# A two-layer decoder trunk: the entries of its feed-forward layers reordered (squares added on VectorE, two raw pairs in layer 1, the first scaled pair's weights of layer 0 held in token tiles)

## The chip, the cores and the metric

One Trainium2 chip, one core of it. The metric is the device time in microseconds (us) of one execution, the median of three runs. Engines: TensorE (PE, with its weight loads PEld), VectorE (DVE), ScalarE (ACT), GpSimd (POOL), SyncE (SP). Each engine works through a queue of its own, in order, and waits on semaphores for the others; most DMAs are issued from SP's queue, some from POOL's.

## The reference, cut to what matters

A residual stream h of 512 tokens by 1024 features goes through two layers. In layer 0 the mixer is a retention and an mLSTM head group (`ab_mixer`), in layer 1 a sparse attention with compressed, selected and window branches (`nsa_mixer`). Each layer then has the same two steps:

```python
for i in range(DEPTH):
    h = h + mixer_i(rms_norm(h, ...), ...)
    h = h + conv_ffn(rms_norm(h, ffn_norm_g[i]), ffn_w_up[i], ffn_conv_w[i], ffn_conv_b[i], ffn_w_down[i])
    e = rms_norm(p[i] @ ple_w[i], ple_norm_g[i])
    gate = sigmoid(rms_norm(h, ple_gate_norm_g[i]) @ ple_w_gate[i])
    h = h + gate * e

def conv_ffn(h, w_up, conv_w, conv_b, w_down):
    a, b = split(h @ w_up, 2)              # 1024 -> 2 x 2816
    a = causal_dwconv(a, conv_w, conv_b)   # width 3 over tokens
    return (gelu(a) * b) @ w_down
```

`rms_norm` divides each token by the root of the mean of its squares, so a product of *unnormalised* (raw) tokens with a weight can be multiplied by the token's factor afterwards.

## The kernel before, in words

Features lie on the partitions, tokens along the free axis: h is eight tiles `self.h[k]` of 128 x 512 (in the trace `hp`, or `h`). Every float32 product is made of three matmuls, `mm3` (L176 to L178): operands are split into a high and a low part, high by a copy on ACT (L136, `split`), low by a subtraction on DVE (L137); then high x high, low x high, high x low go into the same PSUM tile. So each weight tile passes through a raw tile `wr` (four buffers; the load waits until the buffer is free), then `wh` (ACT) and `wl` (DVE). `load` (L159) issues the load under a high priority, and where its caller stands in the code decides together with that priority where it comes in the queues: the order of each engine's queue is worked out ahead of time, by a scheduler that simulates a timeline. `self.behind(engine)` pins an instruction behind the last one traced on that engine. `y` tiles are 28 token tiles of 128 x 512, `sc` tiles six of scratch, `g` tiles twenty in the feed-forward layer.

A norm has these steps: `acc_square` squares each h tile on ACT (L232) and adds it into `acc`, seven adds, six on POOL and the last on DVE (L234); `norm_sum` transposes acc on PE (L310), sums on DVE (L311) and takes an inverse root by small operations (L215 to L221); `norm_cast` spreads it over the partitions by PE (L324) into `n.b` (in the trace `rb`). The raw tokens' parts `norm_parts` are a copy on ACT (L244) and a subtraction on DVE (L245); the normalised tokens are made by `scaled_tokens` (L262 to L275: `fh`, `fl`, `gh`, `gl`, `y`).

**Layer 0, from the mixer into the feed-forward layer.** The mixer's output goes through w_abo in two halves; the second half is eight pieces m of 12 matmuls (`out_piece`, with `out_products`, L370 ff.), and each adds into h[m] on DVE (L373). Ahead of it stand the last head group's products, finished on DVE (L545) after a spread on PE (L324). Behind it `begin` squares and adds h, and fills PE with products of the embedding: p (`pT`, loaded and split in `Embed.fill`) by w_ple, eight pieces of six matmuls, with `norm_sum` after the third and `norm_cast` after the sixth. Then the first pair of up-products (f=0) begins, its two products interleaved with an offset of 2.5 steps.

**Feed-forward layers.** There are 22 blocks f, each a pair of up-products. Blocks below `PLAINS[i]` are plain: 2 x 24 matmuls of 512 columns (`mm_up`). The others (`up`) use a product scheme of seven instead of eight: 84 matmuls of 256 columns, whose operand forms DVE prepares (`forms`) and whose weight sums come by accumulating DMAs from POOL's queue (L1489, L1496: `ep`, `es`; ACT and DVE split the sums into `eh`, `el`). Each block is convolved and gated (`conv`, L1452 to L1455, `act_up`), and groups of blocks (`PARTS`) are multiplied down into h (`down`, L1562).

**Layer 1.** All eight embedding products are done within the attention's steps (750 to 920 us), so at the entry there is nothing to fill with. Instead the first pair (f=0) is multiplied with raw tokens: six of the eight steps of a, `norm_sum`, the others, four steps of b, `norm_cast`, the rest; a is multiplied by `n.b` on DVE (L1466), the gated result once more on POOL (L1469).

**The attention's entry** (633 to 720 us) starts with a norm (`norm_in`), the products of keys, values and gate columns (L803 transposes the gates after L797 on ACT), and the hidden steps of the compressed blocks (L877, L878). In the steps behind it, L1070 to L1126, an order by a planner is interleaved with the output products.

Of the kernel before, what the change touches and what calls it, by code (L numbers as in the profile page):

```python
# [20 lines left out]
P = 128  # L21
# [21 lines left out]
PLAINS = (5, 6)  # L43
# [20 lines left out]
class Trunk:  # L64
# [73 lines left out]


# [96 lines left out]
    def norm_step(self, n, c0, k, place=None):  # L236
        self.norm_parts(n, c0, k, place)
        self.acc_square(n, k, self.h[k])
# [10 lines left out]
    def norm_in(self, c0, place=None):  # L249
        n = Norm()  # L250
        for k in range(KD):
            self.norm_step(n, c0, k, place)
        return n
# [120 lines left out]

    def out_proj(self, src, half, oh, ol):
        for m in range(KD):
            self.out_piece(src, half, m, oh, ol)


    def ab_mixer(self):  # L380
        nc, I, tc = self.nc, self.I, self.tc
        with ExitStack() as ctx:
# [357 lines left out]
            self.out_proj(I["w_abo"], 1, [h for h, _ in mo], [l for _, l in mo])  # L740
        return self.Embed(self, 0, None, self.dram.tile([D, T], F32, name="emb0"), 0)


    def nsa_mixer(self):
# [4 lines left out]
        with ExitStack() as ctx:  # L749
# [18 lines left out]
            n = self.norm_in(C_NSA)  # L768
# [429 lines left out]
            hidden_step(1, xv, ph, 1)  # L1198
            key_stack(1, keys[1])
            q1 = self.Tokens(self, I["w_q"][1], n)  # L1200
            q1.steps(0, 1)
            key_stack(2, keys[2])
# [24 lines left out]
            emb = self.Embed(self, 1, lambda m: self.y().bitcast(F32), self.dram.tile([D, T], F32, name="emb"), KD)  # L1227
# [100 lines left out]
            for m in range(KD):  # L1328
                embed(m, EMBED_AT[m])
                out_first(m, OUT_AT[m])  # L1330
# [32 lines left out]
            for m in range(KD):  # L1363
                if m % 2 == 0:
                    if m // 2 + 4 not in wo:
                        wo[m // 2 + 4] = self.load(I["w_nso"][1, m // 2])
                self.out_add(m, self.out_products(wo[m // 2 + 4], m, *outs[1]))
        return emb


    def ffn(self, i, e):
        nc, I, tc = self.nc, self.I, self.tc
        plain = PLAINS[i]
        with ExitStack() as ctx:
# [23 lines left out]

            def begin():
                self.cycle = ("a", "b")  # L1400
                if e.done == KD:
                    n = Norm()
                    for k in range(KD):
                        self.acc_square(n, k, self.h[k])
                        self.norm_parts(n, C_FFN + 8 * i, k, g_tile)
                    ws = [self.load(I["w_up"][i, x]) for x in (0, NF)]
                    first = [self.bank() for _ in ws]
                    for step, (x, ks) in enumerate(((0, range(6)), (0, range(6, KD)), (1, range(4)), (1, range(4, KD)))):
                        with self.behind(*[nc.tensor] * (step > 0)):
                            for k in ks:  # L1410
                                s = slice(k * P, (k + 1) * P)
                                self.mm3(first[x], ws[x][0][:, s], ws[x][1][:, s], n.h[k], n.l[k], k == 0, k == KD - 1)
                        if step in (0, 2):
                            with self.behind(nc.tensor):
                                (self.norm_sum if step == 0 else self.norm_cast)(n)
                    n.h, n.l = [], []
                    ws = [self.load(I["w_up"][i, x]) for x in (1, NF + 1)]
                    self.scaled_tokens(n, C_FFN + 8 * i, places, whole)
                    return n, ws, first
                n = Norm()  # L1420
                for k in range(KD):
                    self.acc_square(n, k, self.h[k])
                fill = e.fill(g_tile)
                jobs = fill[:3] + [lambda: self.norm_sum(n)] + fill[3:6] + [lambda: self.norm_cast(n)] + fill[6:]
# [3 lines left out]
                ws = [self.load(I["w_up"][i, x]) for x in (0, NF)]  # L1428
                self.scaled_tokens(n, C_FFN + 8 * i, places, whole)
                return n, ws, None  # L1430
# [3 lines left out]
            def mm_up(f):  # L1434
                self.cycle = ("a", "b")
                if f > (first is not None):
                    return self.ws(I["w_up"][i, f], n), self.ws(I["w_up"][i, NF + f], n)
                ps = [self.bank() for _ in ws]
                order = sorted([(k, 0, k) for k in range(KD)] + [(k + 2.5, 1, k) for k in range(KD)])
                for step, (_, x, k) in enumerate(order):  # L1440
                    s = slice(k * P, (k + 1) * P)
                    with self.behind(*[nc.tensor] * (step > 0)):
                        self.mm3(ps[x], ws[x][0][:, s], ws[x][1][:, s], n.h[k], n.l[k], k == 0, k == KD - 1)
                return ps
# [17 lines left out]
            def act_up(f, pa, pb):  # L1462
                raw = first is not None and f == 0
                if raw:
                    a, pa = pa, a_tile()
                    nc.vector.tensor_tensor(pa, a, n.b, ALU.mult)  # L1466
                c = conv(f, pa)
                if raw:
                    nc.gpsimd.tensor_tensor(c, c, n.b, ALU.mult)  # L1469
                nc.vector.scalar_tensor_tensor(c, pb, -1.0, c, ALU.mult, ALU.mult)  # L1470
                keep(f, c)
# [93 lines left out]
            act_up(0, *(first or mm_up(0)))  # L1565
            jobs = []
            for f in range(1, NF):
                if f < plain:
                    if f == plain - 1:
                        with tc.high_priority(offset=AHEAD):  # L1570
                            ahead[0].load()
                            ahead[0].open()
                    act_up(f, *mm_up(f))
                else:
                    up(f)
                if f == 1:
                    forms = self.forms(n)
                if forms:
# [13 lines left out]
    class Embed:  # L1592
        def __init__(self, trunk, i, place, away, done):
            self.k, self.i, self.place, self.away, self.done = trunk, i, place, away, done
            self.n, self.e = Norm(), []

        def fill(self, tile):
            tr = self.k
            src = tr.I["pT"][self.i]
            raw = tr.wp.tile([P, 1024], F32, name=tr.nm("wr"), tag="wr", bufs=4)  # L1600
            self.p = [[tile(), tile()], [tile(), tile()]]
            with tr.tc.high_priority(offset=AHEAD):
                tr.nc.sync.dma_start(raw, src)
                for k in range(2):
                    tr.split(self.p[0][k], self.p[1][k], raw[:, k * T : k * T + T])
            self.place = lambda m: tile().bitcast(F32)
            ws = {}
# [193 lines left out]
```

## Time and profile before

| | |
|---|---|
| median of three runs | 1347.6 us (1346.89 to 1347.86) |
| the profiled execution's own time | 1348.33 us |
| its span, first to last instruction | 1346.5 us |
| mean granted clock of PE | 0.997 |
| PE busy | 1325.0 us, 7826 matmuls |
| DVE, ACT, POOL busy | 1015.0, 739.4, 376.3 us |
| bytes moved by DMA | 171.69 MB, 128 GB/s on average |

The stages by the timeline: the first mixer to about 204 us (its last products run into the entry of the feed-forward layer, first up-product at 239.6), feed-forward layer 0 to 600, its gate to 633, attention to 925, feed-forward layer 1 to 1313, its gate to the end.

How to read it: a line of a timeline has its start, its duration, the engine, the line of the kernel, the operation, output <- inputs, and in brackets how long the engine had been idle and what ended that. "x3" are three in a row. In the list of waits "a <- b" is what waited and what it waited for. Busy times are of the profiled execution.

### The profile page before, as it was taken

The numbers are of one execution on the slowest core, as the hardware profiler recorded it, in microseconds if no ns is written. First come the engines' busy times: TensorE is split into PE (matmuls) and PEld (weight loads), VectorE is DVE, ScalarE is ACT, GpSimd is POOL, SyncE is SP. The second block draws the span as 40 slices with busy tenths as digits, with TensorE's granted clock in tenths as the row PEclk, the third lists the DMA queues.
The fourth block names the chain that finished last, engine by engine and source line by source line (L and its number), as shares of the span: only waits on it lengthen the run. The fifth ranks groups of instructions, "written<-read, shape, count | busy, mean of one in ns | idle before, by whom it ended". The sixth has DMA issues, their size and how long they took to land.

```text
span 1346.5 us, 21190 instructions
## 1 busy us (share of the span) xinstructions
PE 1325.0 (98%) x7826; PEld 1148.3 (85%) x7826; DVE 1015.0 (75%) x1658; ACT 739.4 (55%) x1310; POOL 376.3 (28%) x399
## 2 busy tenths in 40 slices
PE   9999999999999999999999999999899999999998
PEld 7888877789999999888788888887689999999887
DVE  6866866787888877678777878766897788877675
ACT  5357524555555555355466888664454555555342
POOL 3356423011111110331422887673100111110320
PEclk9999999999999999999999999999999999999999
DMA  6532344555666553333243322114255666653421
GB/s 239 159 100 94 110 127 157 176 149 160 173 175 174 145 140 91 129 114 118 85 154 113 111 65 56 28 52 109 83 172 144 169 174 172 164 135 91 133 97 63
DMA packets 72191, 171.69 MB, mean 128 GB/s; under 512 B 8468, under 2 KB 15252, under 8 KB 72088
## 3 DMA queue, kind: packets, MB, share of 16 engines
q1 hardware_dynamic: 62296, 152.91, 35.6%
q0 software_dynamic: 9504, 17.31, 7.8%
q8 instruction: 61, 1.00, 0.3%
q14 instruction: 42, 0.34, 0.1%
q10 hardware_dynamic: 288, 0.14, 0.0%
HBM read 148.29 MB, written 7.35 MB: 116 GB/s over the span
## 4 chain that ended last, share of the span: by engine, by line
PE 91%; DVE 3%; ACT 2%; DMA 1%; issue 1%; POOL 1%; ACTq 0%; POOLq 0%; DVEq 0%
PE ps L176 26%; PE ps L177 26%; PE ps L178 26%; PE ps L1126 3%; PE ps L1101 3%; PE ps L1070 2%; PE ps L1071 1%; DMA es<-in_w_up_dram 1%; ACT wh L136 1%; PE ps L459 1%; DVE wl L137 1%; PE ps L1072 1%; PE ps L310 1%; POOL acc L234 1%; PE ps L996 1%
## 5 line engine op out<-in xcount | busy, mean ns | idle before, releaser
L136 ACT ACTIVATE wh<-wr 128x1024 fp32r<-128x1024 f32 (+2 forms) x182 | 186.7, 1029 | 223.1 <-PE ps L177 169.4
L177 PE MATMUL ps<-y,wh 128*128 128x512 f32 (+1 forms) x752 | 264.2, 352 | 0.2 <-DVE y L137 0.2
L176 PE MATMUL ps<-y,wh 128*128 128x512 f32 (+1 forms) x752 | 263.1, 355 | 1.0 <-ACT y L136 0.9
L178 PE MATMUL ps<-y,wl 128*128 128x512 f32 (+1 forms) x752 | 262.5, 352 | 0.0
L137 DVE TENSOR_TENSOR wl<-wr,wh 128x1024 fp32r<-128x1024 f32 (+2 forms) x165 | 203.0, 1231 | 67.0 <-ACT wh L136 65.9
L176 PEld LDWEIGHTS ps<-y,wh 128*128 128x128 f32 x752 | 142.9, 190 | 22.7 <-ACT y L136 1.6
L177 PEld LDWEIGHTS ps<-y,wh 128*128 128x128 f32 x752 | 142.8, 190 | 19.4 <-DVE y L137 0.6
L178 PEld LDWEIGHTS ps<-y,wl 128*128 128x128 f32 x752 | 142.8, 190 | 18.4
L177 PE MATMUL ps<-g,wh 128*128 128x512 f32 x384 | 150.8, 393 | 2.6 <-DVE g L245 2.6
L176 PE MATMUL ps<-g,wh 128*128 128x512 f32 x384 | 150.9, 393 | 0.0
L178 PE MATMUL ps<-g,wl 128*128 128x512 f32 x384 | 150.0, 391 | 0.0
L1489 POOL DMA_DIRECT2D ep<-ep x33 | 28.4, 861 | 278.4 <-DMA ep<-in_w_up_dram 129.0
L1496 POOL DMA_DIRECT2D es<-in_w_up_dram x33 | 29.0, 887 | 254.6 <-DVE sc L1453 149.7
L177 PEld LDWEIGHTS ps<-g,wh 128*128 128x128 f32 x384 | 72.6, 189 | 17.5 <-DVE g L245 3.9
L234 POOL TENSOR_TENSOR acc<-acc,sc 128x512 f32<-128x512 f32 x36 | 58.1, 1614 | 104.0 <-ACT sc L232 102.9
L1562 DVE TENSOR_TENSOR hp<-hp,ps 128x512 f32<-128x512 f32 x96 | 65.6, 683 | 26.8 <-PE ps L178 26.8
L178 PEld LDWEIGHTS ps<-g,wl 128*128 128x128 f32 x384 | 72.4, 189 | 15.2
L1086 POOL TENSOR_SCALAR pr<-pr,sm,gate 128x512 f32<-128x512 f32 (+3 forms) x128 | 76.4, 614 | 29.5 <-DVE sm L1084 22.5
L176 PEld LDWEIGHTS ps<-g,wh 128*128 128x128 f32 x384 | 72.7, 189 | 14.1
L1529 ACT ACTIVATE sc<-ps 128x256 f32<-128x256 f32 x132 | 50.1, 380 | 60.7 <-PE ps L178 58.8
L176 PE MATMUL ps<-y,gh 128*128 128x256 f32 x264 | 75.0, 284 | 0.0
L178 PE MATMUL ps<-y,fl 128*128 128x256 f32 x264 | 74.8, 283 | 0.0
(366 smaller groups left out, 3388.4 us busy)
## 6 DMA issues: line engine op xcount, KB each, us to landing
wr<-in_w_up_dram SPq DMA_DIRECT2D x55, 512.0 KB, 3.7
ep<-in_w_up_dram SPq DMA_DIRECT2D x33, 512.0 KB, 5.6
wr<-in_w_down_dram SPq DMA_DIRECT2D x64, 256.0 KB, 3.0
es<-in_w_up_dram SPq DMA_DIRECT2D x33, 256.0 KB, 2.9
es<-in_w_up_dram POOLq DMA_DIRECT2D x33, 256.0 KB, 6.4
ep<-ep POOLq DMA_DIRECT2D x33, 256.0 KB, 3.8
wr<-in_w_plg_dram SPq DMA_DIRECT2D x16, 512.0 KB, 3.7
wr<-in_w_down_dram SPq DMA_DIRECT2D x32, 192.0 KB, 2.9
```

What stands on the lines that cost most here:

```text
L136: self.nc.scalar.activation(hi, src, AF.Copy)
L137: (eng or self.nc.vector).tensor_tensor(lo, src, hi.bitcast(F32), ALU.subtract)
L176: mm(out, ah, bh, start=first, stop=False, **kw)
L177: mm(out, ah, bl, start=False, stop=False, **kw)
L178: mm(out, al, bh, start=False, stop=last, **kw)
L234: eng.tensor_tensor(n.acc, n.acc, sq, ALU.add)
L1086: nc.gpsimd.tensor_scalar(prs[b], prs[b], sm[:, b : b + 1], gate[:, j, hd, 1 + b : 2 + b], ALU.mult, ALU.mult)
L1101: nc.tensor.transpose(pt[:, n * w + i * P : n * w + (i + 1) * P], pr[:, n, i * P : (i + 1) * P], self.ident)
L1126: nc.tensor.matmul(po[0:m, cols], vv[i][:, b, g, 0:m], src, start=False, stop=last and b == 1 and i == 0 and part == 0)
L1496: nc.gpsimd.dma_start(me.s3, I["w_up"][i, me.f][:, :T], accum_op=ALU.add)
L1529: copy = lambda out, ps: nc.scalar.activation(out, ps, AF.Copy)
L1562: nc.vector.tensor_tensor(self.h[m], self.h[m], ps, ALU.subtract)
```

## The change

1. **Squares.** `acc_square` gets VectorE for all its adds at the entries of both feed-forward layers and of the attention; POOL no longer adds there. The first mixer and the gates keep POOL.
2. **Layer 0.** Four steps move from the entry in between the pieces of the second half of w_abo (`ahead`): after piece 0 the load and split of pT (`Embed.parts`), after 2 the first half of w_ple (`Embed.weights`), after 4 and 6 the two weights of the first scaled pair (`whole_y`), which are now split into eight y tiles instead of `wh` and `wl`. The first pair is interleaved with an offset of half a step.
3. **Layer 1.** Two pairs (f=0 and 1, `RAW = 2`) are multiplied with raw tokens, their weights loaded by `load_now`. `norm_sum` comes after the second of the four products, `norm_cast` after the third. All four products are multiplied by n.b on DVE. `PLAINS` is (5, 7), so f=6 becomes plain. One embedding product (m=7, `LEFT = 1`) is left for the entry, with pT and w_ple loaded again between the last output products of the attention.
4. **Others.** The forms start four blocks ahead of the first seven-product block; in the attention's entry the gate columns stand behind the first step of q0, and a hidden step behind the first step of q1.

The diff, cut to its core:

```diff
-PLAINS = (5, 6)
+PLAINS = (5, 7)
+RAW = 2
+LEFT = 1
...
+    def whole_y(self, src):
+        raw = self.wp.tile([P, 1024], F32, name=self.nm("wr"), tag="wr", bufs=4)
+        with self.tc.high_priority(offset=AHEAD):
+            self.nc.sync.dma_start(raw, src)
+        halves = []
+        for x in range(2):
+            hi, lo = self.y(), self.y()
+            self.split(hi, lo, raw[:, x * T : x * T + T])
+            halves.append((hi, lo))
+        return [halves[k // 4][c][:, k % 4 * P : k % 4 * P + P] for c in range(2) for k in range(KD)]
...
-            n = self.norm_in(C_NSA)
+            n = self.norm_in(C_NSA, eng=nc.vector)
...
-            self.out_proj(I["w_abo"], 1, [h for h, _ in mo], [l for _, l in mo])
-        return self.Embed(self, 0, None, self.dram.tile([D, T], F32, name="emb0"), 0)
+            e = self.Embed(self, 0, None, self.dram.tile([D, T], F32, name="emb0"), 0)
+            ahead = {0: e.parts, 2: e.weights, 4: lambda: e.up.append(self.whole_y(I["w_up"][0, 0])), 6: lambda: e.up.append(self.whole_y(I["w_up"][0, NF]))}
+            for m in range(KD):
+                self.out_piece(I["w_abo"], 1, m, [h for h, _ in mo], [l for _, l in mo])
+                if m in ahead:
+                    ahead[m]()
+        return e
...
-            gate_columns(sg)
             xv = blocks(1, hT[1])
             q0 = self.Tokens(self, I["w_q"][0], n)
             q0.steps(0, 1)
+            gate_columns(sg)
...
-            emb = self.Embed(self, 1, lambda m: self.y().bitcast(F32), self.dram.tile([D, T], F32, name="emb"), KD)
+            emb = self.Embed(self, 1, lambda m: self.y().bitcast(F32), self.dram.tile([D, T], F32, name="emb"), KD - LEFT)
...
+                if m in (4, 6):
+                    (emb.parts if m == 4 else emb.weights)()
...
             def begin():
                 self.cycle = ("a", "b")
-                if e.done == KD:
-                    n = Norm()
+                n, raw = Norm(), Norm()
+                if e.done:
+                    ws = {}
                     for k in range(KD):
-                        self.acc_square(n, k, self.h[k])
-                        self.norm_parts(n, C_FFN + 8 * i, k, g_tile)
...
+                        self.norm_parts(raw, C_FFN + 8 * i, k, g_tile)
+                        if k == 3:
+                            ws[0, 0] = parts_of(self.load_now(I["w_up"][i, 0]))
+                    for f, x in ((0, 1), (1, 0)):
+                        with self.behind(nc.vector):
+                            ws[f, x] = parts_of(self.load_now(I["w_up"][i, x * NF + f]))
                 for k in range(KD):
-                    self.acc_square(n, k, self.h[k])
...
+                    self.acc_square(n, k, self.h[k], nc.vector)
+                if e.done:
+                    ws[1, 1] = parts_of(self.load_now(I["w_up"][i, NF + 1]))
+                    first = [[self.bank(), self.bank()] for f in range(RAW)]
+                    jobs = [lambda f=f, x=x: up_raw(raw, ws[f, x], first[f][x]) for f in range(RAW) for x in range(2)]
+                    jobs[2:2] = [lambda: self.norm_sum(n)]
+                    jobs[4:4] = [lambda: self.norm_cast(n)]
+                    jobs[:0] = e.fill(lambda: self.sc().bitcast(F32R))
...
-                order = sorted([(k, 0, k) for k in range(KD)] + [(k + 2.5, 1, k) for k in range(KD)])
+                order = sorted([(k, 0, k) for k in range(KD)] + [(k + 0.5, 1, k) for k in range(KD)])
...
+            self.scaled_tokens(n, C_FFN + 8 * i, places, whole)
+            for pair in first:
+                for x, tile in enumerate((a_tile, self.sc)):
+                    t = tile()
+                    with self.behind(nc.vector):
+                        nc.vector.tensor_tensor(t, pair[x], n.b, ALU.mult)
+                    pair[x] = t
...
-                if f == 1:
+                if f == plain - KD // 2:
                     forms = self.forms(n)
```

How the queues come out is shown at three places, in rows of one engine's queue (line, operation, output <- inputs, shape). The first is ACT from the end of the first mixer into layer 0, before: `eh` is the split of a weight sum, `g` the two splits of pT (wr_2079), `y` the token splits of the last head group, the others are weight splits (w_abo's third tile is wr_1983, its fourth wr_2017).

```order
L136 ACTIVATE eh_2730<-es_2602 128x512
L136 ACTIVATE wh_1916<-wr_1915 128x1024
L136 ACTIVATE g_2080<-wr_2079 128x512
L136 ACTIVATE wh_1950<-wr_1949 128x1024
L136 ACTIVATE g_2081<-wr_2079 128x512
L136 ACTIVATE y_1813<-ep_1298 128x512
L136 ACTIVATE y_1843<-ep_1298 128x512
L136 ACTIVATE y_1867<-ep_795 128x512
L136 ACTIVATE wh_1984<-wr_1983 128x1024
L136 ACTIVATE y_1897<-ep_795 128x512
L136 ACTIVATE wh_2018<-wr_2017 128x1024
```

After (w_abo's second, third and fourth tiles are wr_1960, wr_2000 and wr_2044, pT is wr_1936, w_ple wr_1980, the weights of the first scaled pair wr_2020 and wr_2064):

```order
L138 ACTIVATE wh_1961<-wr_1960 128x1024
L138 ACTIVATE y_1813<-ep_1298 128x512
L138 ACTIVATE y_1843<-ep_1298 128x512
L138 ACTIVATE y_1867<-ep_795 128x512
L138 ACTIVATE wh_1981<-wr_1980 128x1024
L138 ACTIVATE y_1897<-ep_795 128x512
L138 ACTIVATE y_1938<-wr_1936 128x512
L138 ACTIVATE y_1939<-wr_1936 128x512
L138 ACTIVATE y_2022<-wr_2020 128x512
L138 ACTIVATE y_2026<-wr_2020 128x512
L138 ACTIVATE y_2066<-wr_2064 128x512
L138 ACTIVATE wh_2001<-wr_2000 128x1024
```

The splits of pT went from ahead of the second w_abo split to behind the token splits, and three of the four splits of the scaled pair's weights stand ahead of the third w_abo split.

The second is DVE at the entry of layer 1, up to the reduction (L311, L333 now) of the norm. Before (`g` are the low parts of raw tokens, `hp` the last output products added into h, `wl` low parts of weights):

```order
L245 SCALAR_TENSOR_TENSOR g_10271<-hp_1691,cols,g_10270 128x512
L373 TENSOR_TENSOR hp_1694<-hp_1694,ps_10215 128x512
L245 SCALAR_TENSOR_TENSOR g_10278<-hp_8772,cols,g_10277 128x512
L245 SCALAR_TENSOR_TENSOR g_10285<-hp_8772,cols,g_10284 128x512
L373 TENSOR_TENSOR hp_1694<-hp_1694,ps_10229 128x512
L245 SCALAR_TENSOR_TENSOR g_10292<-hp_1694,cols,g_10291 128x512
L137 TENSOR_TENSOR wl_10394<-wr_10392,wh_10393 128x1024
L234 TENSOR_TENSOR acc_10247<-acc_10247,sc_10295 128x512
L245 SCALAR_TENSOR_TENSOR g_10299<-hp_1694,cols,g_10298 128x512
L311 TENSOR_REDUCE tiny_10335<-ps_10334 128x4
```

After:

```order
L395 TENSOR_TENSOR hp_1694<-hp_1694,ps_10243 128x512
L256 TENSOR_TENSOR acc_10311<-acc_10311,sc_10322 128x512
L267 SCALAR_TENSOR_TENSOR g_10292<-hp_1694,cols,g_10291 128x512
L256 TENSOR_TENSOR acc_10311<-acc_10311,sc_10325 128x512
L267 SCALAR_TENSOR_TENSOR g_10296<-hp_1694,cols,g_10295 128x512
L139 TENSOR_TENSOR wl_10301<-wr_10299,wh_10300 128x1024
L139 TENSOR_TENSOR wl_10307<-wr_10305,wh_10306 128x1024
L256 TENSOR_TENSOR acc_10311<-acc_10311,sc_10328 128x512
L139 TENSOR_TENSOR wl_10336<-wr_10334,wh_10335 128x1024
L256 TENSOR_TENSOR acc_10311<-acc_10311,sc_10331 128x512
L333 TENSOR_REDUCE tiny_10403<-ps_10402 128x4
```

Adds into `acc` came in between the others, and three weight splits stand next to each other ahead of the last two.

The third is PE in the attention's entry, at the transposes of the gates, before:

```order
L176 MATMUL ps_6443<-wh_6570,y_6288 128x512
L176 MATMUL ps_6444<-wh_6570,y_6288 128x512
L176 MATMUL ps_6445<-wh_6570,y_6288 128x512
L176 MATMUL ps_6446<-wh_6570,y_6288 128x512
L803 MATMUL ps_6666<-ident,sc_6438 128x48 x4
L177 MATMUL ps_6443<-wl_6571,y_6288 128x512
```

After:

```order
L198 MATMUL ps_6451<-wh_6578,y_6296 128x512
L198 MATMUL ps_6452<-wh_6578,y_6296 128x512
L198 MATMUL ps_6453<-wh_6578,y_6296 128x512
L198 MATMUL ps_6454<-wh_6578,y_6296 128x512
L826 MATMUL ps_6725<-ident,sc_6446 128x48 x4
L199 MATMUL ps_6451<-wl_6579,y_6296 128x512
```

The gate columns stand behind a step of q0 in the code, and in PE's queue where they stood.

More of the change, by code (lines that the diff above doesn't have):

```diff
@@ L137, in split, with load_now @@
         (eng or self.nc.vector).tensor_tensor(lo, src, hi.bitcast(F32), ALU.subtract)
+    def whole_y(self, src):
[8 more added lines that the diff above has]
+        return [halves[k // 4][c][:, k % 4 * P : k % 4 * P + P] for c in range(2) for k in range(KD)]
+    def load_now(self, src):
+        raw = self.wp.tile([P, 1024], F32, name=self.nm("wr"), tag="wr", bufs=4)
+        hi = self.wp.tile([P, 1024], F32R, name=self.nm("wh"), tag="wh")
+        lo = self.wp.tile([P, 1024], F32R, name=self.nm("wl"), tag="wl")
+        with self.tc.high_priority(offset=AHEAD):
+            self.nc.sync.dma_start(raw, src)
+        self.split(hi, lo, raw)
+        return hi, lo
     def load_late(self, src):
@@ L1328, in nsa_mixer @@
             for m in range(KD):
-                embed(m, EMBED_AT[m])
+                if m < emb.done:
+                    embed(m, EMBED_AT[m])
                 out_first(m, OUT_AT[m])
@@ L1403, in begin @@
                     for k in range(KD):
-                        self.acc_square(n, k, self.h[k])
-                        self.norm_parts(n, C_FFN + 8 * i, k, g_tile)
[L1406 to L1415, printed above, removed]
@@ L1427, in begin, with up_raw @@
                         f()
-                ws = [self.load(I["w_up"][i, x]) for x in (0, NF)]
-                self.scaled_tokens(n, C_FFN + 8 * i, places, whole)
-                return n, ws, None
+                if e.done:
+                    ws = [parts_of(self.load(I["w_up"][i, x])) for x in (RAW, NF + RAW)]
+                return n, ws, first
+            def up_raw(raw, w, ps):
+                for k in range(KD):
+                    term(ps, w, raw, k)
             gt = {}
@@ L1564, in ffn @@
             n, ws, first = begin()
-            act_up(0, *(first or mm_up(0)))
+            self.scaled_tokens(n, C_FFN + 8 * i, places, whole)
[5 more added lines that the diff above has]
+                    pair[x] = t
             jobs = []
-            for f in range(1, NF):
+            for f in range(NF):
                 if f < plain:
@@ L1594, in __init__, with parts, weights @@
             self.k, self.i, self.place, self.away, self.done = trunk, i, place, away, done
-            self.n, self.e = Norm(), []
+            self.n, self.e, self.up = Norm(), [], []
+        def parts(self):
+            tr = self.k
+            raw = tr.wp.tile([P, 1024], F32, name=tr.nm("wr"), tag="wr", bufs=4)
+            with tr.tc.high_priority(offset=AHEAD):
+                tr.nc.sync.dma_start(raw, tr.I["pT"][self.i])
+            self.p = [[tr.y(), tr.y()], [tr.y(), tr.y()]]
+            for k in range(2):
+                tr.split(self.p[0][k], self.p[1][k], raw[:, k * T : k * T + T])
+        def weights(self):
+            self.w = self.k.load_now(self.k.I["w_ple"][self.i, self.done // 4])
         def fill(self, tile):
             tr = self.k
[L1599 to L1605, printed above, removed]
             self.place = lambda m: tile().bitcast(F32)
-            ws = {}
+            ws = {self.done // 4: self.w}
             def one(m):
```

46 lines of the change are left out of this document (19 added, 27 removed).

## The prediction

> **What bounds the kernel now.** I read the page first, then the waits of TensorE (PE), then the stretches in which PE waits: their clock by windows, and the timelines of the engines that PE waits for. The page:
>
> ```profile
> span 1346.5 us, 21190 instructions
> PE 1325.0 (98%) x7826; PEld 1148.3 (85%) x7826; DVE 1015.0 (75%) x1658; ACT 739.4 (55%) x1310; POOL 376.3 (28%) x399
> PE 91%; DVE 3%; ACT 2%; DMA 1%; issue 1%; POOL 1%; ACTq 0%; POOLq 0%; DVEq 0%
> ```
>
> PE is busy for 98% of the span and holds 91% of the chain that ended last. So a change pays only where PE waits, where its clock is halved, or where it gets less work. Its waits, as "PE line <- engine that ended the wait: us in total, times, longest":
>
> ```profile
> PE ps L310 <- DVE acc L234: 3.3, 2, 2.3
> PE ps L324 <- DVE ep L545: 3.0, 1, 3.0
> PE ps L177 <- DVE g L245: 2.6, 3, 1.1
> PE ps L178 <- DVE wl L137: 1.6, 2, 0.8
> PE ps L176 <- ACT y L136: 0.9, 1, 0.9
> PE ps L803 <- ACT sc L797: 0.7, 1, 0.7
> PE ps L177 <- DVE fl L269: 0.6, 2, 0.4
> ```
>
> All of these stand at entries of layers. After two of them the granted clock is down to half. Per stretch the windows give PE's busy time and its number of matmuls (x), then the other engines, then the clock:
>
> ```profile
> core 0: us, PE busy (x) PEld busy (x) DVE busy (x) ACT busy (x) POOL busy (x), PEclk, DMA share, GB/s
> 204.20:207.60 3.40, 3.23 (x8) 2.55 (x9) 3.40 (x6) 1.76 (x3) 0.00 (x0) 0.51 0.61 213
> 207.60:211.00 3.40, 3.40 (x16) 2.81 (x15) 0.86 (x2) 0.00 (x0) 0.86 (x1) 0.99 0.57 178
> 934.00:948.00 14.00, 9.48 (x39) 6.58 (x37) 13.36 (x13) 8.57 (x14) 10.16 (x7) 1.00 0.40 106
> 948.30:951.70 3.40, 3.38 (x10) 2.89 (x11) 2.48 (x9) 0.10 (x1) 0.00 (x0) 0.51 0.49 154
> ```
>
> In 3.40 us PE starts 8 matmuls at clock 0.51 and 16 at 0.99, so a half-clock window costs 1.7 us beside the wait that brought it. The pitch of a 512-column matmul at full clock is 0.227 us: in the two rows below lie twelve pitches in 2.72 us (columns: start, us, what).
>
> ```profile
> 937.71 0.39 PE L176 MATMUL ps<-y,wh 128*128 128x512 f32 x1
> 940.43 0.39 PE L176 MATMUL ps<-g,wh 128*128 128x512 f32 x1
> ```
>
> **Entry of layer 0 (part 2 of the change).** The wait of 3.0 us, seen from ACT, DVE and PE:
>
> ```profile
> 189.74 0.63 ACT L136 ACTIVATE eh<-es 128x512 fp32r<-128x512 f32 x1 [7.96 <-DMA es<-in_w_up_dram]
> 197.88 0.63 ACT L136 ACTIVATE g<-wr 128x512 fp32r<-128x512 f32 x1 [6.56 <-DMA wr<-in_pT_dram]
> 198.42 1.04 ACT L136 ACTIVATE wh<-wr 128x1024 fp32r<-128x1024 f32 x1
> 201.84 1.28 DVE L545 TENSOR_TENSOR ep<-ep,ps 128x512 f32<-128x512 f32 x2
> 202.57 0.65 PE L324 MATMUL ps<-ident,tiny 128*128 128x128 f32 x4 [2.96 <-DVE ep L545]
> ```
>
> ACT stands 6.56 us on the split of pT, which PE needs only after the out-projection, and a weight split that PE needs at once is queued behind it; DVE's splits follow, then L545, then PE. The change issues pT's load ahead of the last three w_abo loads, and its splits stand behind the four y splits. ACT then takes that weight split at about 191 and L545 ends by 199, when PE arrives (199.4). The 3.0 us and the 1.7 us of half clock behind them go: **-4.7**. The scaled pair's weights are now split long before their use, so one of the two waits on wl goes too, at 243: **-0.8**.
>
> In their place comes a wait that the trace of before doesn't have. The loads and splits of w_up stand ahead of the third w_abo split on ACT and on DVE, in order. The first w_up tile takes the slot that pT's splits free: counting DVE's operations from L545 (eleven of 0.64 to 1.23 us), about 206. How long such loads take:
>
> ```profile
> wr<-in_w_up_dram SPq DMA_DIRECT2D x55, 512.0 KB, 3.7
> es<-in_w_up_dram POOLq DMA_DIRECT2D x33, 256.0 KB, 6.4
> ```
>
> At 3.7 us the tile lands at 210; four loads of 512 KB are released within a microsecond or two, so the second may land as late as 212.5. Then follow y (0.6), wh (1.04) and wl (1.2), and PE has its pieces at 212 to 215. It wants them at 211 to 212: 199.4, the transposes, and 48 matmuls of 0.227 us (10.9). The new wait is 0.7 to 3.3 us; I take **+2.0**, near the middle, since two loads overlap. If it is over 2 us it may bring back the half clock, 1.7 more: the waits of 3.0 and 2.26 us did, those of 1.1 us and less did not.
>
> The Trainium skill ("TensorE: Matmul & The Clock Gate", What's actually happening) has the clock halve after an idle window of about 3.4 us that runs freely; this trace shows it after waits of 3.0 and 2.26 us that follow stutters. By the page's figure alone the new wait would never bring it, and the sum would keep +2.0; by the rows it can.
>
> **Entry of layer 1 (parts 1 and 3).** DVE, POOL and PE there:
>
> ```profile
> 932.86 1.22 DVE L137 TENSOR_TENSOR wl<-wr,wh 128x1024 fp32r<-128x1024 f32 x1
> 937.42 2.77 DVE L137 TENSOR_TENSOR wl<-wr,wh 128x1024 fp32r<-128x1024 f32 x1
> 942.39 2.88 DVE L245 SCALAR_TENSOR_TENSOR g<-hp,cols,g 128x512 fp32r<-128x512 f32 x2
> 945.79 0.74 DVE L245 SCALAR_TENSOR_TENSOR g<-hp,cols,g 128x512 fp32r<-128x512 f32 x1
> 947.59 0.68 DVE L234 TENSOR_TENSOR acc<-acc,sc 128x512 f32<-128x512 f32 x1
> 933.12 3.83 POOL L234 TENSOR_TENSOR acc<-acc,sc 128x512 f32<-128x512 f32 x2 [5.54 <-ACT sc L232]
> 937.49 5.53 POOL L234 TENSOR_TENSOR acc<-acc,sc 128x512 f32<-128x512 f32 x3
> 929.80 0.63 ACT L136 ACTIVATE eh<-es 128x512 fp32r<-128x512 f32 x1 [2.16 <-DMA es<-in_w_up_dram]
> 948.32 1.11 PE L310 MATMUL ps<-ident,acc 128*128 128x128 f32 x4 [2.26 <-DVE acc L234]
> ```
>
> While POOL adds squares, the same weight split takes 2.77 instead of 1.22 us, and two L245 take 2.88 instead of 1.48. Moving the six adds to DVE costs DVE 6 x 0.68 = 4.1 us and gives back most of the stretch (1.5 + 1.4 from these two rows, about 4.7 in all): nearly even. What decides is the second piece: two raw products (48 matmuls, 10.9 us) now stand ahead of the norm's transposes L310, where 21 stood. From DVE's new order I get acc at about 951.7, and PE at L310 at about 953. So 2.3 (acc), 2.6 (g), 0.9 (y, filled by 15 matmuls that don't need it), 0.4 (fl), 0.8 (wl) and 1.7 of half clock go: **-8.7**. What stays is that g's pairs come one after the other at DVE's pace: three waits of 0.5, 0.6 and 0.25 us in that walk, **+1.3** (0 to 2.6, the sum of before). The second raw pair fills PE until the norm is cast. The four multiplications by the norm (DVE, 0.68 each) replace one on DVE and one on POOL; 24 raw matmuls (5.4 us) stand behind the cast on PE and cover them.
>
> The Trainium skill ("SBUF — State Buffer", Reading the diagram under SBUF: two separate sides) calls the port that DVE and POOL share an exclusive lock, held for a whole instruction. The trace agrees: 2.77 is 1.22 and about one POOL add. The same page warns that DVE may keep POOL from writing descriptors of its own DMAs, which speaks against this change; no run here shows it.
>
> ACT and DVE now have the split of es (L136 eh) ahead of a w_nso split. If es lands as before (row at 929.80), the w_nso split ends at 931.3, and PE comes to it at about 934: I cost it at nothing, with a cover of 2.7 us; a landing later than that is paid in full.
>
> **One scaled pair more, one product of seven less.** For f=6 the plain form is 48 matmuls of 512 columns (48 x 0.227 = 10.9), the seven-product form 84 of 256 (9.5 by columns). The conversions L1452 mark the blocks:
>
> ```profile
> L1452 ACT ACTIVATE sc<-ps,cols x1: 668/668/668, 999.1 to 999.1; 128x512 f32<-128x512 f32 x1
> L1452 ACT ACTIVATE sc<-ps,cols x1: 672/672/672, 1013.9 to 1013.9; 128x512 f32<-128x512 f32 x1
> L1452 ACT ACTIVATE sc<-a,cols x1: 705/705/705, 1032.4 to 1032.4; 128x512 f32<-128x512 f32 x1
> L1452 ACT ACTIVATE sc<-a,cols x1: 709/709/709, 1046.5 to 1046.5; 128x512 f32<-128x512 f32 x1
> ```
>
> A plain block with its share of down-products takes 14.8, a seven-product one 14.1: **+0.8** (0.7 to 1.4). The embed product m=7 (6 matmuls, 1.4 us) moves out of the attention steps into the entry: less there, more here, **0** (0 to +1.4).
>
> **Entry of the attention layer.**
>
> ```profile
> 634.79 9.32 POOL L234 TENSOR_TENSOR acc<-acc,sc 128x512 f32<-128x512 f32 x6 [39.20 <-ACT sc L232]
> 644.99 0.63 PE L310 MATMUL ps<-ident,acc 128*128 128x128 f32 x4 [1.03 <-DVE acc L234]
> ```
>
> On DVE the six adds are 4.1 us in place of 9.3, acc is ready by 642: **-1.0**. The gate columns and one hidden step move in the code, but PE's order there stays row for row, so the waits on L797 and on a weight split stay: 0. The attention steps behind (750 to 920) come out in another order; PE hardly waits there, and I give it 0 with 3 us to either side.
>
> **Sum:** -4.7 - 0.8 + 2.0 - 8.7 + 1.3 + 0.8 - 1.0 = -11.1 on the profiled execution, which took 1348.3 (1.8 outside its span) and lies 0.7 over the median of 1347.6. The forecast is 1337.2 by the profile, **1336.5** by the median.
>
> **Rivals.** *DVE takes the bound (slower).* From 934 to 948 DVE is busy 13.36 of 14.00 us. If its operations stay as long as they were, whatever POOL does, the 4.1 us of adds and 2 us of further multiplications lie on the path, and the waits of before stay: 6.1 + 0.8 - 3.5 (layer 0) = +3.4, 1351. It decides from acc being 1.3 us later than I walked; beyond, each us is paid. For it: the 13.36. Against: 1.22 and 0.74 as soon as POOL rests. 0.09.
>
> *The new wait in layer 0 halves the clock again:* 3.3 + 1.7 in place of 2.0, 1339.5. For it: four loads together. 0.17.
>
> *The gain is given back:* the attention steps in their new order eat 3, es lands 3 us late behind DVE's adds and brings 1.7, and the waits on g stay at 2.6: +9, near 1345.5 to 1347.5, no change. 0.06.
>
> *Every wait goes and none comes:* without the +2.0 and +1.3, and with the steps 2 us better, 1331. 0.14.
>
> The forecast itself has 0.54.
>
> **How the numbers follow.** The range takes in the forecast, the half clock and the better case, with 3 us of the steps: 1330 to 1343; the slower case, the given-back case and about 0.04 of tails are left out. A measurement of this kernel tells 0.2% (2.7 us) from no change. Faster by more: 0.54 + 0.17 + 0.14 and a little of the given-back case, 0.87. Within: 0.04. Slower: the first rival, 0.09.
>
> **What would show it.** Right: no wait of L346 (L324 now) on L563 near 199 and clock 1.0 there; a wait on wh or wl of w_abo near 212, under 3.3 us; DVE's splits of 1.2 us through the entry of layer 1, no wait of L332 (L310 now) on acc, the first scaled pair of layer 1 (f=2) starting near 965 less what the stages before gained. Wrong: clock 0.5 near 215 or 950, DVE still over 13 of 14 us ahead of the norm with PE waiting for acc, or more than 3 us of new waits between 750 and 920.

## The result and the profile after

The changed kernel takes 1337.2 us (median of six runs, 1335.93 to 1340.91) against 1346.99 before: a ratio of 0.993, 95% interval 0.9917 to 0.9943, 9.8 us less. (The kernel before was measured beside every group of runs below; its medians lie between 1346.99 and 1347.62, so medians of different groups compare to about 0.6 us.) The profiled execution is the slowest of its six, 1340.91 us; why, stands below. Its page:

```profile
span 1339.2 us, 21105 instructions
PE 1325.0 (99%) x7790; PEld 1146.1 (86%) x7790; DVE 1018.9 (76%) x1676; ACT 737.9 (55%) x1309; POOL 342.6 (26%) x378
PE 93%; DVE 4%; ACT 1%; DMA 1%; issue 1%; ACTq 0%; DVEq 0%
```

PE is as busy as before (with a half clock in it) in a span 7.3 us shorter. Its waits after:

```profile
PE ps L198 <- ACT wh L138: 4.1, 4, 1.6
PE ps L199 <- DVE g L267: 1.2, 2, 0.9
PE ps L200 <- DVE wl L139: 0.9, 1, 0.9
PE ps L826 <- ACT sc L820: 0.5, 1, 0.5
PE ps L198 <- DVE hp L395: 0.2, 1, 0.2
```

The waits on acc (3.3) and on ep (3.0) are gone, those on g are halved. A wait on weight splits on ACT has grown from 1.2 to 4.1; before, it was this one:

```profile
PE ps L176 <- ACT wh L136: 1.2, 1, 1.2
```

Where the span changed, by the starts of the same PE instructions in both timelines:

| PE starts | before | after | change since the row above |
|---|---|---|---|
| layer 0, spread L324 / L346, first of four | 202.57 | 199.34 | -3.2 |
| first product on scaled tokens (`fh`) | 239.58 | 240.26 | +3.9 |
| first on a weight sum (`eh`) | 305.7 | 304.9 | -1.5 |
| attention, norm's transposes | 644.99 | 643.01 | -1.2 |
| its last value product (`pt`, `vv`) | 922.3 | 916.2 | -4.1 |
| layer 1, norm's transposes | 948.32 | 949.17 | +6.9 |
| first product on scaled tokens | 958.08 | 961.0 | +2.1 |
| end | 1346.5 | 1339.2 | -10.2 |

The last four rows have moved work in them: 16 matmuls of 512 columns (3.6 us, six of them the embedding product) went from ahead of the last value product to behind it, 48 raw matmuls stand ahead of layer 1's transposes where 18 did (6.8 us more), and a seven-product block became plain. PE's lost time, the stretch minus its matmul columns at 0.227 us per 512, is free of that: from the last value product to the first `eh` it is 11.8 us before and 5.8 after.

Layer 0 first. ACT and PE at the third w_abo split:

```profile
203.28 2.18 ACT L138 ACTIVATE y<-wr 128x512 fp32r<-128x512 f32 x4
212.20 0.63 ACT L138 ACTIVATE y<-wr 128x512 fp32r<-128x512 f32 x1 [6.73 <-DMA wr<-in_w_up_dram]
212.73 1.04 ACT L138 ACTIVATE wh<-wr 128x1024 fp32r<-128x1024 f32 x1
213.82 0.50 PE L198 MATMUL ps<-y,wh 128*128 128x512 f32 x1 [1.60 <-ACT wh L138]
215.94 0.79 PE L200 MATMUL ps<-y,wl 128*128 128x512 f32 x1 [0.91 <-DVE wl L139]
```

The wait near 199 is gone, and this one has taken its place: ACT stands 6.73 us on the second w_up tile, the w_abo split right behind it, PE behind that. The load of that w_abo tile is not what is late; it was issued at 194.0 and took 3.7 us:

```profile
L181 SPq DMA_DIRECT2D wr<-in_w_abo_dram x1: 328/328/328, 194.0 to 194.0; - x1
DMA to landing us min/median/max: 3.7/3.7/3.7
```

Then the clock (columns as in the windows of before):

```profile
core 0: us, PE busy (x) PEld busy (x) DVE busy (x) ACT busy (x) POOL busy (x), PEclk, DMA share, GB/s
208.00:215.00 7.00, 5.40 (x23) 3.85 (x21) 2.83 (x5) 2.80 (x5) 0.00 (x0) 1.00 0.56 164
215.30:222.10 6.80, 6.16 (x15) 4.81 (x16) 5.51 (x9) 3.13 (x6) 0.00 (x0) 0.50 0.74 251
222.20:229.00 6.80, 6.80 (x32) 5.60 (x31) 4.39 (x6) 2.24 (x4) 0.00 (x0) 1.00 0.30 92
930.00:948.00 18.00, 16.77 (x69) 12.58 (x70) 17.45 (x24) 12.51 (x19) 0.86 (x1) 1.00 0.56 165
```

For 6.8 us, two windows of 3.4, the clock is halved and PE starts 15 matmuls, against 32 in the 6.8 us behind: half of it, 3.4 us, is lost in this execution. In the other five of the six the mean clock was 0.999 or 1.000 against 0.997 here, and the times were 2.8 to 5.0 us lower. (In the profiles of this case a mean clock of 0.999 or 1.000 goes with no half-clock window between the kernel's start and its end, 0.998 with one, 0.997 with two.)

Layer 1, DVE, ACT and PE:

```profile
932.77 1.42 DVE L267 SCALAR_TENSOR_TENSOR g<-hp,cols,g 128x512 fp32r<-128x512 f32 x2
946.75 0.69 DVE L256 TENSOR_TENSOR acc<-acc,sc 128x512 f32<-128x512 f32 x1
949.80 0.69 DVE L333 TENSOR_REDUCE tiny<-ps 128x4 f32<-128x512 f32 x1 [2.35 <-PE ps L332]
926.17 0.63 ACT L138 ACTIVATE eh<-es 128x512 fp32r<-128x512 f32 x1 [6.63 <-DMA es<-in_w_up_dram]
929.89 0.50 PE L198 MATMUL ps<-y,wh 128*128 128x512 f32 x1 [0.38 <-ACT wh L138]
949.17 0.38 PE L332 MATMUL ps<-ident,acc 128*128 128x128 f32 x2
1014.05 0.50 PE L198 MATMUL ps<-fh,wh 128*128 128x512 f32 x1 [0.97 <-ACT wh L138]
```

From 930 to 948 DVE is busy 17.45 of 18.00 us, and still PE doesn't wait for acc: it is ready at 947.4, and PE comes at 949.17. Two low parts of raw tokens take 1.42 us with POOL at rest (2.88 before). Small waits are new: 0.21 and 0.38 behind the split of es, and 0.97 at 1014.

### The profile page after: what moved, and what is told of

It is laid out like the page before. It is cut to its first block, busy times and chain, and to the rows that moved or that the text cites. A ratio compares the mean times of both kernels' runs of the same rounds, so it can differ in the third digit from the quotient of the medians.

```text
span 1339.2 us, 21105 instructions
## 1 busy us (share of the span) xinstructions
PE 1325.0 (99%) x7790; PEld 1146.1 (86%) x7790; DVE 1018.9 (76%) x1676; ACT 737.9 (55%) x1309; POOL 342.6 (26%) x378
## 4 chain that ended last, share of the span: by engine, by line
PE 93%; DVE 4%; ACT 1%; DMA 1%; issue 1%; ACTq 0%; DVEq 0%
PE ps L198 26%; PE ps L200 26%; PE ps L199 26%; PE ps L1149 3%; PE ps L1124 3%; PE ps L1093 2%; PE ps L1094 1%; DVE wl L139 1%; PE ps L477 1%; PE ps L1095 1%; PE ps L332 1%; PE ps L1019 1%; PE ps L1042 1%; DMA wr<-in_w_up_dram 0%; ACT wh L138 0%
## 5 line engine op out<-in xcount | busy, mean ns | idle before, releaser
L1098 ACT ACTIVATE pr<-ps,nmx 128x512 f32<-128x512 f32 (+3 forms) x128 | 68.3, 545 | 10.7 <-DVE nmx L1096 10.0
L198 PE MATMUL ps<-y,fh 128*128 128x256 f32 x256 | 72.4, 283 | 0.0
```

The costliest lines, as they stand in the source:

```text
L198: mm(out, ah, bh, start=first, stop=False, **kw)
L1098: nc.scalar.activation(pr[:, b], s[:, b], AF.Exp, bias=nmx[:, b : b + 1], accum_out=sm[:, bs[b] : bs[b] + 1])
```

## The experiments

**Part 2 undone.** pT, w_ple and the first pair's weights at the entry again:

```diff
-            ahead = {0: e.parts, 2: e.weights, 4: ..., 6: ...}
+            ahead = {}
...
+                    with tc.high_priority(offset=AHEAD):
+                        nc.sync.dma_start(raw, I["pT"][i])
+                        for k in range(2):
+                            self.split(e.p[0][k], e.p[1][k], raw[:, k * T : k * T + T])
```

> The changed kernel with the layer-0 part undone: pT, w_ple and the first scaled pair's weights are loaded and split at the entry again, pT's splits under the load's priority, the pair at its old offset. Theory (the part pays through the pT wait): the 3.0 us wait and its half clock come back, and the wait on wl at 243, while the waits of 3.2 us on the third w_abo split go. From PE's lost time per stage (17.3 us before, 13.3 after without the half clock of the profiled execution) the time is 1341.3, 4.1 over the changed kernel. Rival (the part only moves waits, as the first up-product at 240.3 instead of 239.6 suggests): 1337 to 1338.

Measured 1340.4 us, 0.9947 of before (0.9935 to 0.996): 3.2 over the changed kernel. ACT and PE:

```profile
195.87 0.63 ACT L138 ACTIVATE g<-wr 128x512 fp32r<-128x512 f32 x1 [6.22 <-DMA wr<-in_pT_dram]
200.56 0.43 PE L346 MATMUL ps<-ident,tiny 128*128 128x128 f32 x2 [1.91 <-DVE ep L563]
```

pT's split holds ACT again and PE waits, 1.91 here. The part pays; the rival is out.

**Only the place of pT's splits.** As above, but without the load's priority on the splits:

```diff
+                    e.parts()
+                    e.weights()
```

> As the layer-0 part undone, but pT's splits do not carry the load's priority, so they stand behind the four token splits on ACT; w_up is still split at the entry. Theory (all of the 3.0 + 1.7 us comes from the place of pT's two splits in ACT's queue): no wait near 199, none near 212, the wait on wl at 243 stays: 1341.3 - 4.7 = 1336.6 or a little less. Rival (the earlier load of pT is what counts): the wait near 199 stays, 1341.

Measured 1335.8 us, 0.9913 (0.99 to 0.9927): 4.6 us under the undone part, and 1.4 under the changed kernel. ACT goes straight through:

```profile
191.85 1.06 ACT L138 ACTIVATE wh<-wr 128x1024 fp32r<-128x1024 f32 x1 [0.58 <-ACT wh L138]
237.88 0.50 PE L200 MATMUL ps<-fh,wl 128*128 128x512 f32 x1 [0.82 <-DVE wl L139]
```

The whole gain of 4.6 us was to be had by the place of two instructions in ACT's queue: up to 211 us nothing else changes place there against the undone part. The wait on wl is what the early weights remove.

**The w_up splits behind the w_abo splits.**

```diff
-            ahead = {0: e.parts, 2: e.weights, 4: <w_up 0>, 6: <w_up NF>}
+            ahead = {0: e.parts, 2: e.weights, 6: <w_up 0>, 7: <w_up NF>}
...
+            with self.behind(self.nc.scalar):
                 self.split(hi, lo, raw[:, x * T : x * T + T])
```

> The changed kernel with the two loads of the first scaled pair issued after pieces 6 and 7 of w_abo instead of 4 and 6, and their splits pinned behind the weight splits of w_abo on ACT. Theory (the splits of w_up that wait for their load hold the w_abo split behind them): the waits of 1.76, 1.08 and 0.36 us between 212 and 216 go, and the half clock behind them with them: 1334, clock 1.0 in all of layer 0. Rival (the w_abo split is late by its own load, or the pair's weights then come late at 237): 1337, with a wait of a like size elsewhere.

Measured 1334.6 us, 0.9909 (0.9896 to 0.9923), 2.6 under the changed kernel. The stretch behind 208 now:

```profile
core 0: us, PE busy (x) PEld busy (x) DVE busy (x) ACT busy (x) POOL busy (x), PEclk, DMA share, GB/s
208.00:215.00 7.00, 7.00 (x33) 5.79 (x32) 7.00 (x11) 6.66 (x11) 0.00 (x0) 1.00 0.63 187
215.30:222.10 6.80, 6.80 (x32) 5.63 (x31) 5.91 (x9) 2.62 (x4) 0.00 (x0) 1.00 0.83 263
```

33 matmuls where there were 23, clock 1.00 throughout in this execution. The new wait was the price of part 2's order, not of its loads: the second w_up tile is loaded here at nearly the same time (issued at 205.4 against 205.7, 5.7 us to landing against 6.4), and no wait comes of it.

**Squares back on POOL, two raw pairs kept.**

```diff
-            n = self.norm_in(C_NSA, eng=nc.vector)
+            n = self.norm_in(C_NSA)
...
-                    self.acc_square(n, k, self.h[k], nc.vector)
+                    self.acc_square(n, k, self.h[k])
```

> The changed kernel with the squares' adds back on GpSimd at the three entries. Theory (the adds on GpSimd delay acc at the attention's entry and stretch VectorE's operations at layer 1's, while two raw products cover acc there): 1.2 us at 643 come back, 1 to 2 us of waits on g at 941 to 946 are added, no wait on acc in layer 1: 1339.5. Rival (VectorE is the bound at the entries, 4.1 us less work on it pays): 1335 to 1336.

Measured 1342.0 us, 0.9962 (0.995 to 0.9975): 4.8 over the changed kernel, more than the 2.3 expected. To have layer 0's clock out of it, the same edit on the kernel with the w_up splits behind:

> The kernel with the w_up splits behind the w_abo splits, squares' adds back on GpSimd at the three entries. Theory (with two raw pairs the adds on GpSimd cost 1.2 at the attention's entry, about 2.5 of waits in layer 1 and there 1.7 of half clock): 1334.6 + 5.4 = 1340. Rival (as the squares alone, put on VectorE before, were worth under 1 us, most of the 4.8 us seen was layer 0's clock): 1336.

Measured 1339.8 us, 0.9944 (0.9931 to 0.9956): 5.2 over that kernel, as expected (5.4). DVE and POOL there:

```profile
924.46 0.75 DVE L268 SCALAR_TENSOR_TENSOR g<-hp,cols,g 128x512 fp32r<-128x512 f32 x1
926.86 3.27 DVE L268 SCALAR_TENSOR_TENSOR g<-hp,cols,g 128x512 fp32r<-128x512 f32 x2
932.29 3.46 DVE L268 SCALAR_TENSOR_TENSOR g<-hp,cols,g 128x512 fp32r<-128x512 f32 x2
926.23 8.98 POOL L257 TENSOR_TENSOR acc<-acc,sc 128x512 f32<-128x512 f32 x5
```

Beside POOL's adds two low parts take 3.3 us, otherwise 1.5. With the pairs so late PE waits for g and for weights, and a half clock comes with it (0.998 in most runs).

**Squares on DVE alone, on the kernel before.** The edit is the one above the other way round, in the kernel before.

> The kernel before with only the squares' adds moved to VectorE at the three entries. Theory (GpSimd's adds delay acc and stretch VectorE's operations beside them): 1.2 us at 644 go, VectorE's splits at 934 to 946 take 1.2 us instead of up to 2.8, waits on g shrink from 2.6 to about 1.2, and the wait on acc in layer 1 shrinks from 2.3 to at most 1.5: 1343.5, 3.5 less than before. Rival (VectorE is the bound there, and only a second raw pair covers its 4.1 us more): 1346 to 1348, acc later than 948.3.

Measured 1346.5 us, 0.9995 (0.9986 to 1.0003): 0.9 us less by the median, not clear of no change, and my theory (3.5 less) fell. The rival has the time right, but not its sign: acc is ready at 947.1, before 948.3 and not after. DVE and PE at the norm, then two windows:

```profile
944.96 2.14 DVE L234 TENSOR_TENSOR acc<-acc,sc 128x512 f32<-128x512 f32 x3
947.15 0.47 PE L310 MATMUL ps<-ident,acc 128*128 128x128 f32 x1 [4.61 <-DVE acc L234]
```

```profile
934.00:947.00 13.00, 8.54 (x38) 6.75 (x36) 12.89 (x19) 8.19 (x13) 0.86 (x1) 0.96 0.49 142
946.00:952.80 6.80, 5.65 (x16) 4.59 (x17) 4.83 (x16) 1.06 (x1) 0.00 (x0) 0.50 0.01 2
```

The waits on g (2.6 us) are gone, as expected. But PE then only arrives earlier at the norm, and waits 4.61 us for acc in place of 2.26: acc is 1.2 us earlier, no more, since DVE is busy 12.89 of 13.00 us, with 19 operations (before: 13 in 14 us). In this execution two half-clock windows follow instead of one. So this entry gains next to nothing: from the last value product to the first `eh` PE lost 11.5 us, against 11.8 before. The attention's entry gained what was expected (PE lost 1.2 us less there). That the profiled execution is only 0.4 us shorter comes from 1.0 us more lost ahead of the first of the moved adds: 0.5 in the first 16 us, the rest in a longer wait on ep (3.42).

**One raw pair.**

```diff
-PLAINS = (5, 7)
-RAW = 2
+PLAINS = (5, 6)
+RAW = 1
```

`norm_sum` then stands behind the first raw product, `norm_cast` behind the second.

> The changed kernel with one raw pair and 6 plain blocks in layer 1 (squares on VectorE, layer 0 and the embedding product m=7 as changed). Theory (24 more raw matmuls ahead of the norm cover acc, and 24 behind it the norm's chain): PE comes to the norm's transposes 5.4 us earlier and waits 3.7 us for acc, a half clock of 1.7 follows, and 2 to 4 us of waits on fl, since the scaled tokens can't be ready earlier; 0.8 us less work: 1337.2 + 3.7 + 1.7 + 3 - 0.8 = 1344.8. Rival (the squares on VectorE alone made layer 1's gain): 1336 to 1338.

Measured 1347.5 us, 1.0001 (0.9991 to 1.0011): 10.3 over the changed kernel, 2.7 more than expected. The list of waits:

```profile
PE ps L332 <- DVE acc L256: 3.9, 1, 3.9
PE ps L198 <- ACT fh L285: 3.1, 1, 3.1
```

Both waits are as foreseen; the rest is half clock, three windows in layer 1 in the profiled execution (mean clock 0.995). That execution has full clock in layer 0 and spans 1343.9 us, against 1335.8 for the changed kernel's less its 3.4 of half clock: 8.1 us more, near the 7.6 expected. From the last value product to the first `eh` PE lost 13.8 us, against 5.8. The other executions have a mean clock of 0.993 to 0.995, which means more half-clock windows in most of them; where these lie no profile shows, so the 2 us by which the median is further off can't be put down to the raw pair.

**No product left for the entry.**

```diff
-LEFT = 1
+LEFT = 0
...
-                if m in (4, 6):
-                    (emb.parts if m == 4 else emb.weights)()
```

> The changed kernel with all eight embedding products in the attention's steps again, pT and w_ple not loaded twice. Theory (the product is six matmuls wherever it stands, and at the entry g's pairs set the pace): 1.4 us more in the steps, 1.4 less at the entry, of which the waits on g take back up to 1.4: 1337.2 to 1338.6. Rival (the steps have room beside PE, the entry does not): 1335.8.

Measured 1335.2 us, 0.9916 (0.9903 to 0.993): the rival's time. The wait at 1014 goes too. On the kernel with the w_up splits behind:

> The kernel with the w_up splits behind the w_abo splits, and all eight embedding products in the attention's steps. Theory (the product left for the entry costs 1.3 us, with the wait on a weight at 1012 that comes with it; the two repairs don't touch each other): 1334.6 - 1.3 = 1333.3. Rival (the gain seen with all eight products was the half clock of layer 0, which that execution had for one window and the changed kernel's profile for two): 1334.6.

Measured 1333.0 us, 0.9893 (0.9879 to 0.9906): 1.6 less than without. Of the rival's reason one half holds: in these two kernels PE lost 2.65 us less from the last value product to the first `eh`, but 0.75 more in the attention behind its entry, so the steps do not take the product for nothing. Why the wait at 1014 comes with the left product stays open. A late load it is not: ACT's split that PE waits for starts at 1012.94, and the last w_up load ahead of it was issued at 996.5, where such a load takes 3.6 us in the median.

**Six plain blocks.** `PLAINS = (5, 6)` alone:

> The changed kernel with 6 plain blocks in layer 1 as before, two raw pairs kept. Theory (a plain block costs 0.75 us more than one of seven products, and nothing else depends on it): 1336.4; the wait of 1.1 us on a weight at 1012 goes with it if it belongs to the swap: then 1335.3. Rival (the forms of the seven-product blocks come too late with one plain block less): over 1338, with waits on the forms near 1015.

Measured 1339.8 us, 0.9941 (0.9928 to 0.9953). This says nothing of the blocks: four of its five executions have a mean clock of 0.997, the profiled one from layer 0's wait; the fifth (0.998) took 1336.3. It does say that the wait on a weight is not the swap's, as it stays (0.92 at 998.74). So once more, with that wait repaired and no product left:

> As the one before, and 6 plain blocks in layer 1 instead of 7. Theory (a block of seven products is 0.6 to 0.8 us cheaper, without the half clock of layer 0 in the way): 1332.6. Rival (the forms come late with one block less in front): no gain, 1333.3 or more, with waits on forms or weights after 1000.

Measured 1330.4 us, 0.9874 (0.9861 to 0.9888), 2.6 less, where 0.7 was expected. From the first product on scaled tokens in layer 1 to the end PE takes 375.45 us instead of 376.28: 0.8 is the block. The rest of the 2.3 us between the two profiled executions lies ahead of it: 0.3 before layer 0's first scaled product, 0.6 in the attention behind its entry, and 0.6 at layer 1's entry, where the waits on g shrink from 0.5 to 0.15. Why the order came out better there was not tested. Its waits:

```profile
PE ps L199 <- ACT wh L138: 1.1, 1, 1.1
PE ps L199 <- ACT y L138: 0.9, 1, 0.9
PE ps L827 <- ACT sc L821: 0.5, 1, 0.5
```

This is the fastest version: no wait on acc, ep or wl left in the list, and 7 us under the changed kernel.

**The moved gate columns and hidden step.** Both back at their old places:

> The kernel with the w_up splits behind the w_abo splits, the gate columns and the hidden step in the attention's entry back at their old places in the code. Theory (PE's queue stands as it did, so nothing moves): 1334.6. Rival (other queues differ, and the wait of 1.3 us on a weight near 703 or that on the gates near 659 changes): 1 us to either side.

Measured 1334.95 us, 0.9907 (0.9892 to 0.9922), against 1334.59: nothing, and the wait near 704 is there in both (1.20 and 1.11).

## Why the prediction was right, point by point

The forecast was 1336.5 by the median, 1337.2 came. As a difference the forecast was 11.1 us (from 1347.6) and 9.8 came (from 1346.99); between the spans of the profiled executions it is 7.3, and 10.7 without the 3.4 of half clock in layer 0. The mechanisms stood, the sizes less well:

- *Layer 0's wait on ep and its clock (-4.7):* right, the wait is gone and the clock full there. With the place of the two splits alone, 4.6.
- *The wait on wl (-0.8):* right, and a wait of 0.23 on fl went with it; PE lost 1.45 us less between the first `fh` and the first `eh`.
- *The new wait (+2.0, 0.7 to 3.3):* its place and its cause were right, the second w_up tile landing at 212.1 (212.5 as the latest in the walk). The walk of the first tile was wrong: it was not loaded at 206 but at 197.3, and its splits ran at 204.32, ahead of any wait. The size of the wait is 1.60 + 0.91, and 2.6 by the median of the kernel without it.
- *The rival of a halved clock (0.17):* it happened in the profiled execution with two windows (3.4 us; I had 1.7), and by their mean clock in none of the other five. Taken as a case that is either so or not, it was put wrongly: it is a chance per execution, as the last section shows.
- *Layer 1 (-8.7 + 1.3 = -7.4):* the term that was mis-sized: PE lost 6.0 us less there. acc in time with 1.7 us to spare (I had 1.3), the half clock gone, 1.2 left on g: as walked. What failed is "I cost it at nothing" for the split of es: PE came 6 us earlier than before and es only 3.6, so the cover was used up (waits of 0.21 and 0.38). es was issued 5.8 us earlier, but took 6.1 us to land where it had taken 3.9. The squares on DVE are not why: it takes 6.1 with them on POOL too, and 3.8 with them on DVE in the kernel before. What made it slower is not shown. The wait of 0.97 at 1014 was not foreseen.
- *What decides there:* the step said that squares on DVE are nearly even by themselves and that the second raw pair decides. (18 raw matmuls stood ahead of the norm before, not 21 as I wrote.) The runs show more than that: the squares alone are worth 0.9 us, not clear of nothing (0.9995), and neither of the two can be taken from the changed kernel: without the squares 5.2 us are lost, without the second pair 8.1 in the profiled execution. From the last value product to the first `eh` PE lost 11.8 us before, 11.5 with the squares alone, 10.3 with the second pair alone and 5.8 with both (in it one, two, one and no half-clock window). The pair needs DVE's short operations for its operands, the squares need the pair as cover.
- *DVE as the bound (0.09):* half right as a mechanism. DVE is full (17.45 of 18.00), and without the second pair PE waits for it; with it, it doesn't.
- *The block (+0.8):* right, 0.8. *The left product (0 to +1.4):* 1.6 and 2.0 in the two pairs of kernels, outside. *The attention's entry (-1.0):* 1.2.

That the median came so near has some luck in it: layer 1 gave 1.4 us less than forecast, while layer 0 without the half clock gave 0.7 more, PE lost 0.5 less in the attention behind its entry, and 0.2 less at the entry; and the kernel before came out 0.6 us faster than the forecast took it to be.

## What to carry to other kernels

In an in-order queue, ask of every early load what its *split* stands in front of: the gain and the new loss of layer 0 both came from one waiting copy ahead of a weight that was needed at once, and both could be had right by order alone. Work taken off one engine can move the wait to the next join, as the squares alone did here (2.26 us on acc became 4.61); it paid with work to cover that join, so two such edits have to be tried together before either is dropped. Compare medians of many runs when PE idles for about half of a window of 3.4 us, and read from the profile whether the clock halved.

## What the runs showed of the hardware

The half clock depends on more than the wait. Three kernels have nearly the same wait at 212 to 216 (1.7 to 2.3 us on wh, then 0.3 to 0.9 on wl). Their windows, in the order: one raw pair, six plain blocks, no product left:

```profile
215.30:222.10 6.80, 6.30 (x28) 5.22 (x29) 6.70 (x11) 4.19 (x7) 0.00 (x0) 1.00 0.75 267
```

```profile
215.50:222.30 6.80, 6.10 (x14) 4.79 (x15) 5.51 (x9) 3.20 (x6) 0.00 (x0) 0.50 0.75 250
```

```profile
215.00:218.40 3.40, 3.08 (x8) 1.97 (x7) 3.40 (x5) 3.40 (x7) 0.00 (x0) 0.50 0.19 48
```

None, two and one window of 3.4 us, with no order by the length of the wait. What decides is where the wait falls. In each of the 14 profiles all changes of the granted clock lie on one grid of 3.413 us that runs through the whole execution: in the kernel before the clock fell at 204.23 and at 948.34, 744.11 us or 218.0 windows apart. Where the grid starts differs from execution to execution. Here is the grid window with the wait, of the changed kernel, six plain blocks, no product left and one raw pair, each cut along its own grid:

```profile
211.93:215.34 3.41, 1.49 (x6) 0.68 (x4) 2.48 (x4) 3.14 (x6) 0.00 (x0) 1.00 0.08 34
212.05:215.46 3.41, 1.44 (x6) 0.67 (x4) 2.34 (x4) 3.00 (x5) 0.00 (x0) 1.00 0.02 10
211.61:215.02 3.41, 1.15 (x6) 0.62 (x4) 1.33 (x3) 2.00 (x3) 0.00 (x0) 1.00 0.26 99
211.38:214.80 3.42, 1.69 (x7) 0.83 (x5) 2.07 (x4) 2.74 (x5) 0.00 (x0) 1.00 0.04 16
```

In the first three PE is busy for 1.15 to 1.49 us, and the next window is at half clock. In the last it is busy for 1.69, because the grid parts the wait on wh from the one on wl, and the clock stays. Over all windows at full clock in the 14 profiles, by the profile's busy times of PE: the next one was at half clock in 20 of 20 cases where PE was idle for 1.9 us or more (13 of them at the kernel's end), in 5 of 10 with 1.5 to 1.9 us, and in none of 5409 with less. Within the kernel a half-clock window was followed by another where PE was busy for 0.83 of it or less (four cases), and by full clock where it was busy for 0.90 or more.

The Trainium skill ("TensorE: Matmul & The Clock Gate", What's actually happening) says that the window of activity is free-running, so that the turn depends on where in it the work falls; the traces agree, by the grid. They do not agree with an idle window of about 3.4 us as the condition: 1.92 us of idleness in one window, waits of 1.6 us and part of 0.9, was enough in the profiled execution of the changed kernel. The prediction took the Trainium skill's length for the rule, and the rows' lengths for a threshold; both leave out the phase.
